# Start of a hybrid decoder layer: bias product and two more matmuls among the warm-up work, the later rows' norm right behind their sums, row copies on ScalarE, some low weights on GpSimd

## The chip, the cores and the metric

The kernel runs on one core of a Trainium2 chip. The metric is the time of one execution on the device in microseconds (us). The engines are TensorE (PE in the profile; PEld is its weight load), VectorE (DVE), ScalarE (ACT), GpSimd (POOL) and SyncE (SP), which issues most of the DMAs.

## The reference

One inference step of a decoder layer on 512 prompt rows and 32 sample rows (8 sequences of 4), each 1024 wide, in fp32:

```python
h = rmsnorm(x, norm_mix_pre)
xr, q, k, v, g = split(h @ w_in)              # 1024, 1024, 256, 256, 2048 columns
lru  = rg_lru(causal_conv4(xr))               # gated linear recurrence
attn = window_attention(q, k, v)              # window 128, 8 query heads, 2 kv heads, sinks,
                                              # relative bias rel_bias[bucket(distance)]
m = (sigmoid(g_lru) * (lru @ w_lru_o) + sigmoid(g_attn) * (attn @ w_attn_o)) @ w_out
x = x + rmsnorm(m, norm_mix_post)
u = causal_conv3(rmsnorm(x, norm_ffn_pre) @ w_up)
x = x + rmsnorm((gelu(u_gate) * u_val) @ w_down, norm_ffn_post)
```

It also returns the layer's states, among them the last 128 rows of `k` and `v`.

## The kernel before

Activations lie transposed, channels on the partitions and the 544 rows along the free axis, in two column halves: a = 0 is columns 0 to 255, a = 1 columns 256 to 543. Every fp32 product is made of three in a shorter format: each operand is split into a high and a low part (`hH`, `hL`; `wh`, `wl`), and `mm` multiplies high by high, high weight by low activation, and low weight by high activation. The high part is written by ScalarE, the low part is the difference, which VectorE makes as a rule. One product of 128 output channels takes 24 such matmuls.

A weight block of 1024 x 128 (`wload`, on SyncE's queue) is split in two halves of 128 x 512, called units; `wsplit_hi` (L278) and `wsplit_lo` (L283) make their parts. The helper `tick` orders the work around each product. Once per product it takes, in this order: the high parts of the next units (ScalarE), the side generators that are due (`sides`), the results of the product before (`todo`), the low parts of the units, and what stands in `last`. All engines work through what is issued to them in program order. `start_at(t, gen)` lets a generator begin at tick t; each `yield` ends its share of a tick.

How the kernel starts:

- SyncE loads the rows of `x` (five tiles of up to 128 rows, each in two halves of 512), gains and weights. The tables for the relative bias, `relx` (33 x 8) and the one-hot `ohp` (33 x 384), come behind the third weight block.
- TensorE runs WARM = 12 dummy products of `ones` and `ident`, transposes one gain vector (`ps_rows_a0`), and runs KEEP = 11 more dummies, while rows 0 to 255 of `x` arrive. `xsquares` sums their squares (ScalarE one half, VectorE the other), `xrstd` makes the reciprocal root of the mean with one Newton step on VectorE, `scale0` scales the rows.
- The rows are transposed into four PSUM tiles `ps_ta`; `hsplit` writes `hH` and `hL` from them, and the first product (`first_mm`, `pm_first`) follows piece by piece. Its two low weights are made by GpSimd.
- Then come products of the first five weight blocks with a = 0 (k and v of the first kv head, three query heads), and the same five with a = 1.
- The generator `norm_b` prepares the later rows, 256 to 543, from tick 1 on. In its first tick it puts `xsquares(2..4)` and the copies `keep_a(0..3)` into `last`; in its second `keep_a(4..7)`, `xrstd(2, 5)` and the scaling `xscale`; in its third and fourth it transposes into eight PSUM tiles `ps_tb`, and leaves `hsplit` and `keep_b` of each to the tick after. `keep_a` and `keep_b` copy the normed rows from PSUM to SBUF (`xn`), turn about on VectorE and ScalarE; the rows are needed again after the mixer.
- The generator `attn_tables` multiplies `relx` by `ohp` in tick 2 (`ps_ohp`), copies the result (`rvec`, VectorE) in tick 3 and writes it to DRAM (`rscr`, on GpSimd's DMA queue). `load_rep` replicates it in DRAM (`rrep`) for each pair of heads in ticks 4, 6, 13 and 20, and `load_btab` loads the skewed bias tables (`btab`) in ticks 5, 10, 17 and 26; both are issued by GpSimd.

Later, `v_done` (L692 to L694) copies each kv head's `v` from PSUM on ScalarE and its last 32 columns to `vn` on GpSimd; `sample_rows` transposes `kn` and `vn` (`pkn`, L778 and L779) in tick 19 for the attention of the sample rows. `put_away` writes `xn` to DRAM from GpSimd's queue from tick 13 on.

PSUM holds two pools of tiles of 128 x 512 floats: three for products (`PM`) and five for everything else (`PX`).

Of the kernel before, what the change touches and what calls it, by code (L numbers as in the profile page):

```python
# [11 lines left out]
F32 = mybir.dt.float32  # L12
# [5 lines left out]
P = 128  # L18
D = 1024
KD = D // P  # L20
SEQ = 512
# [3 lines left out]
NT = SEQ + NS  # L25
# [99 lines left out]
def hawk_step(ctx, tc, I, O):  # L125
# [69 lines left out]
    def tick(target=0, dt=1):  # L195
        now[0] += dt
        todo = late[:]
        late.clear()
        split = [wsplit_hi(u) for u in wclaim(target)]
        sides()  # L200
        for f in todo:
            f()
        for u in split:
            wsplit_lo(*u)
        for f in last:
            f()
        last.clear()
# [145 lines left out]
    def xload(i):  # L353
        t0, n, src = TOK[i]
        for z in range(2):
            xt[i, z] = S(f"x{i}_{z}")
            nc.sync.dma_start(out=xt[i, z][:n, 0:512], in_=src[:, 512 * z:512 * z + 512])

    xload(0)
    nc.sync.dma_start(out=rows_a[0:8, :], in_=I["norm_mix_pre"].rearrange("o (k p) -> (o k) p", p=P))  # L360
# [6 lines left out]
    wload(2)  # L367
    relx = cp.tile([NBK + 1, NH], F32, name="relx")
    pool.memset(relx, 1.0)
    nc.sync.dma_start(out=relx[0:NBK, :], in_=I["rel_bias"])  # L370
    ohp = T("ohp")[:NBK + 1, 0:3 * WIN]
    nc.sync.dma_start(out=ohp, in_=I["c_ohp"])
    for r, nme in ((8, "norm_mix_post"), (16, "norm_ffn_pre"), (24, "norm_ffn_post")):
# [4 lines left out]

    pw = PX("ps_warm")
    ps0 = PX("ps_rows_a0")  # L380
    for z in range(WARM):
        mm(pw[:, (z % 4) * P:(z % 4 + 1) * P], ones, ident, True, True)
    pe.transpose(ps0[:, 0:8], rows_a[0:8, :], ident[0:8, 0:8])
    for z in range(KEEP):
        mm(pw[:, (z % 4) * P:(z % 4 + 1) * P], ones, ident, True, True)
    G_PRE, G_POST, G_FPRE, G_FPOST, C_W, C_B, C_BR, C_BI, C_LAM = 0, 8, 16, 24, 32, 64, 72, 80, 88
# [69 lines left out]
    for z, k in enumerate(seq + (None,) * 3):  # L456
# [7 lines left out]
        if z == 1:  # L464
            wsplit_lo(*wsplit_hi(u1), eng=pool)
        if 2 <= z < KD + 2:
            first_mm(seq[z - 2], 0, 0, start=z == 2)
# [8 lines left out]
    rmsd = drp.tile([5, P], F32, name="rmsd")  # L476

    def keep_a(k):
        (dve.tensor_copy if k % 2 else act.copy)(xn[k][:, 0:256], ps_ta[k // 2][:, k % 2 * 256:k % 2 * 256 + 256])

    def keep_b(k, ps):
        (act.copy if k % 2 else dve.tensor_copy)(xn[k][:, 256:NT], ps[:, :288])

# [7 lines left out]
    def norm_b():  # L491
        last.extend(lambda i=i: xsquares(i) for i in (2, 3, 4))
        last.extend(lambda k=k: keep_a(k) for k in range(4))
        yield
        last.extend(lambda k=k: keep_a(k) for k in range(4, KD))
        last.append(lambda: xrstd(2, 5))
        last.extend(lambda i=i, e=e: xscale(i, e) for i, e in ((2, "av"), (3, "av"), (4, "vv")))
        yield
        for k in range(KD):
            ps = PX(f"ps_tb{k}")  # L500
            for i in (2, 3, 4):
                t0, n, _ = TOK[i]
                pe.transpose(ps[:, t0 - 256:t0 - 256 + n], xtile(i, k), ident[:n, :n])
            late.append(lambda k=k, ps=ps: (hsplit(k, 1, ps[:, :288]), keep_b(k, ps)))
            if k in (3,):
# [181 lines left out]
    def v_done(kv, a, ps):  # L687
# [5 lines left out]
        if a == 1:  # L693
            pool.tensor_copy(vn[:, kv, :], v[:, SEQ:NT])  # L694
            start_at(now[0] + 1, v_tok(kv, v))
# [266 lines left out]
    start_at(13, put_away())  # L962
    start_at(2, attn_tables())
    start_at(9, params())
# [933 lines left out]
```

## Time and profile before

| | |
|---|---|
| median of 3 runs | 1001.81 us (1001.38 to 1003.03) |
| the profiled execution | 1000.44 us |
| its span, first to last instruction | 998.6 us |
| TensorE busy in the span | 986.9 us |
| VectorE, ScalarE, GpSimd busy | 733.4, 578.1, 166.9 us |
| mean granted clock of TensorE | 0.999 |

The span is what the views of the profile divide up; 1.84 us of the execution lie outside it. Busy times overlap, so a busy engine need not set the time. In a row of the timeline the first figure is the start in us from the start of the span, the second the time until the end of the last instruction of the group (back-to-back instructions overlap, so starts tell the pace); then follow the engine, the line in the kernel, the operation, what it writes and reads, its size, the count, and in brackets the idle time ahead of it and what ended it. Line numbers are often those of a helper (L166 is every matmul made by `mm`), so the names tell the step.

### The profile page before, as it was taken

Reading aid. Unit: us, or ns where it says so; the run is one execution under the profiler, and the core shown is the slowest. Engines: PE = TensorE matmul, PEld = TensorE weight load, DVE = VectorE, ACT = ScalarE, POOL = GpSimd, SP = SyncE. Lnnn points to the kernel's source line nnn. Section 1 sums busy time; section 2 is a strip of 40 time slices with the busy share of each in tenths; the row PEclk is TensorE's granted clock in tenths of the full one; section 3 lists DMA queues with packets and bytes.
Section 4 is the critical chain, followed back from the end, with each engine's and each line's share of the span. In section 5 each row is a group of like instructions: output and inputs, shape, how many; then the busy total and the mean of one; then the engine's idle time right before and its main releaser. Section 6 shows DMA issues by size and latency. Waiting matters only on the chain.

```text
span 998.6 us, 20168 instructions
## 1 busy us (share of the span) xinstructions
PE 986.9 (99%) x7807; PEld 975.4 (98%) x7807; DVE 733.4 (73%) x1541; ACT 578.1 (58%) x1411; POOL 166.9 (17%) x279
## 2 busy tenths in 40 slices
PE   8999999999999999999999999999999999999997
PEld 7899999999999999999999999999999999999996
DVE  6566688545945656589777788888888888888765
ACT  6544455469448625556676756565656565656652
POOL 1152011001404463210001111111111111011004
PEclk9999999999999999999999999999999999999999
DMA  7756323322323634326256768676767676768612
GB/s 210 181 134 220 96 64 103 109 85 70 113 72 99 193 97 137 90 85 200 63 117 132 186 128 190 132 185 131 187 137 181 139 179 143 175 139 210 196 45 90
DMA packets 212114, 135.93 MB, mean 136 GB/s; under 512 B 9544, under 2 KB 197721, under 8 KB 211988
## 3 DMA queue, kind: packets, MB, share of 16 engines
q1 hardware_dynamic: 200052, 113.04, 39.8%
q0 software_dynamic: 11920, 19.59, 12.0%
q10 hardware_dynamic: 48, 2.03, 0.7%
q8 instruction: 61, 1.00, 0.4%
q14 instruction: 33, 0.27, 0.1%
HBM read 112.10 MB, written 11.37 MB: 124 GB/s over the span
## 4 chain that ended last, share of the span: by engine, by line
PE 92%; DVE 3%; ACT 3%; DMA 1%; issue 0%; SPq 0%; POOL 0%; ACTq 0%; DVEq 0%
PE pmin L166 21%; PE pmdn L166 17%; PE pux L1449 16%; PE puy L1449 8%; PE pq L1449 6%; PE pmout L166 5%; PE pmlo L166 5%; PE pmao L166 5%; PE puz L1449 4%; PE pg L166 1%; PE psc L166 1%; PE pvp L166 1%; PE pt L744 1%; PE ptok L166 1%; DMA x<-in_x_prompt_dram 1%; ACT wh_in L278 0%
## 5 line engine op out<-in xcount | busy, mean ns | idle before, releaser
L166 PE MATMUL pmin<-hH,wh_in 128*128 128x256 f32 (+1 forms) x568 | 166.0, 292 | 0.0
L166 PE MATMUL pmin<-hH,wl_in 128*128 128x256 f32 (+1 forms) x568 | 163.4, 288 | 0.4 <-DVE wl_in L283 0.4
L166 PE MATMUL pmin<-hL,wh_in 128*128 128x256 f32 (+1 forms) x568 | 163.7, 288 | 0.0
L166 PE MATMUL pmdn<-fH,wh_dn 128*128 128x256 f32 (+1 forms) x448 | 129.4, 289 | 0.2 <-DVE ft L175 0.2
L166 PE MATMUL pmdn<-fH,wl_dn 128*128 128x256 f32 (+1 forms) x448 | 129.1, 288 | 0.0
L166 PE MATMUL pmdn<-fL,wh_dn 128*128 128x256 f32 (+1 forms) x448 | 129.0, 288 | 0.0
L178 DVE SCALAR_TENSOR_TENSOR uc<-u,fv,uc 128x560 f32<-128x560 f32 x128 | 102.0, 797 | 13.3 <-ACT uc L1480 13.2
L166 PEld LDWEIGHTS pmin<-hH,wh_in 128*128 128x128 f32 x568 | 107.2, 189 | 1.9 <-issue 1.2
L166 PEld LDWEIGHTS pmin<-hH,wl_in 128*128 128x128 f32 x568 | 106.9, 188 | 0.7 <-DVE wl_in L283 0.6
L166 PEld LDWEIGHTS pmin<-hL,wh_in 128*128 128x128 f32 x568 | 107.0, 188 | 0.0
L166 PEld LDWEIGHTS pmdn<-fH,wh_dn 128*128 128x128 f32 x448 | 84.4, 188 | 0.6 <-issue 0.6
L166 PEld LDWEIGHTS pmdn<-fH,wl_dn 128*128 128x128 f32 x448 | 84.4, 188 | 0.0
L166 PEld LDWEIGHTS pmdn<-fL,wh_dn 128*128 128x128 f32 x448 | 84.4, 188 | 0.0
L1575 ACT COPY u<-pux 128x272 f32<-128x272 f32 x52 | 20.0, 385 | 83.8 <-PE pux L1449 83.8
L169 DVE TENSOR_TENSOR u<-puy,u 128x240 f32<-128x240 f32 (+2 forms) x78 | 24.6, 344 | 48.9 <-PE puy L1449 32.0
L175 DVE TENSOR_TENSOR ft<-ft,pmdn 128x256 f32<-128x256 f32 (+1 forms) x104 | 45.4, 437 | 17.0 <-PE pmdn L166 16.6
L278 ACT ACTIVATE wh_in<-raw_in 128x512 fp32r<-128x512 f32 x72 | 44.2, 628 | 17.6 <-PE pmin L166 6.1
L1480 ACT ACTIVATE uc<-u,fv 128x560 f32<-128x560 f32 x64 | 48.3, 755 | 0.0
L283 DVE TENSOR_TENSOR wl_in<-raw_in,wh_in 128x512 fp32r<-128x512 f32 x70 | 46.9, 684 | 0.8 <-ACT wh_in L278 0.7
L707 ACT ACTIVATE s<-s,st 128x256 f32<-128x256 f32 (+1 forms) x32 | 15.2, 475 | 50.1 <-DVE st L704 37.4
L1375 POOL DMA_DIRECT2D raw_up_s<-raw_up_s x26 | 22.7, 872 | 101.1 <-DMA raw_up_s<-raw_up__10513 4.5
L169 DVE TENSOR_TENSOR wl_dn<-raw_dn,wh_dn 128x512 fp32r<-128x512 f32 x56 | 38.4, 685 | 0.0
(782 smaller groups left out, 3427.6 us busy)
## 6 DMA issues: line engine op xcount, KB each, us to landing
raw_in<-in_w_in_dram SPq DMA_DIRECT2D x36, 512.0 KB
raw_dn<-in_w_down_dram SPq DMA_DIRECT2D x56, 256.0 KB
raw_up_s<-in_w_up_dram SPq DMA_DIRECT2D x25, 512.0 KB
raw_up_s<-raw_up_s POOLq DMA_DIRECT2D x26, 256.0 KB, 5.7
raw_ao<-in_w_attn_o_dram SPq DMA_DIRECT2D x8, 512.0 KB
raw_lo<-in_w_lru_o_dram SPq DMA_DIRECT2D x8, 512.0 KB
raw_out<-in_w_out_dram SPq DMA_DIRECT2D x8, 512.0 KB
xdram<-xn POOLq DMA_DIRECT2D x8, 272.0 KB, 14.0
```

The lines of the kernel that those rows point to most:

```text
L166: pe.matmul(out, l, r, start=start, stop=stop)
L169: dve.tensor_tensor(out=out, in0=a, in1=b, op=ALU.subtract)
L175: dve.tensor_tensor(out=out, in0=a, in1=b, op=ALU.add)
L178: dve.scalar_tensor_tensor(out=out, in0=a, scalar=s_, in1=b, op0=op0, op1=op1)
L278: act.activation(hl[0], raw, AF.Copy)
L283: (eng or dve).tensor_tensor(out=hl[1], in0=raw, in1=f32(hl[0]), op=ALU.subtract)
L707: act.activation(s3[:, j, :], s3[:, j, :], AF.Exp, bias=ng[:, j:j + 1], accum_out=sm[:, j:j + 1])
L744: pe.transpose(pt[:, (2 * ch + j) * P:(2 * ch + j + 1) * P], s3[:, j, ch * P:(ch + 1) * P], ident)
L1375: pool.dma_start(out=w["p4"], in_=w["p2"], accum_op=ALU.add)
L1449: pe.matmul(ps[:, :HN], w, x, start=start and k == 0 and i == 0, stop=stop and k == 3 and i == 2, skip_group_check=True)
L1480: act.activation(yt[j][:, 0:FLATU], u[:, 0:FLATU], AF.Copy, scale=fv[:, j:j + 1])
L1575: act.copy(e[nm_], z)
```

## The change

- The tables `relx` and `ohp` are loaded ahead of `x`, on ScalarE's DMA queue. Their product `ps_ohp` is issued right behind the gain transpose, ahead of the second group of dummies. The dummies' PSUM tile comes from the pool of products.
- Two more dummies are issued in the first product, ahead of its first matmul.
- In `norm_b`, `xrstd` and `xscale` move from the second tick to the end of the first, behind `keep_a(0..3)`. `attn_tables`, now a plain function, copies `rvec` on ScalarE and issues the write of `rscr` in the first tick as well, ahead of those copies.
- `keep_a` runs on ScalarE alone. `keep_b` runs after each group of four `hsplit`, the first two of a group on ScalarE and the other two on VectorE.
- In ticks 1 to 6 the second unit's low part is made by GpSimd.
- `vn` is copied by ScalarE.

```diff
@@ tick
-        for u in split:
-            wsplit_lo(*u)
+        for z, u in enumerate(split):
+            wsplit_lo(*u, eng=pool if z and now[0] <= 6 else None)
@@ the loads and the dummies
+    relx = cp.tile([NBK + 1, NH], F32, name="relx")
+    pool.memset(relx, 1.0)
+    act.dma_start(out=relx[0:NBK, :], in_=I["rel_bias"])
+    ohp = T("ohp")[:NBK + 1, 0:3 * WIN]
+    act.dma_start(out=ohp, in_=I["c_ohp"])
     xload(0)
...
     wload(2)
-    relx = cp.tile([NBK + 1, NH], F32, name="relx")
-    pool.memset(relx, 1.0)
-    nc.sync.dma_start(out=relx[0:NBK, :], in_=I["rel_bias"])
-    ohp = T("ohp")[:NBK + 1, 0:3 * WIN]
-    nc.sync.dma_start(out=ohp, in_=I["c_ohp"])
...
-    pw = PX("ps_warm")
+    pw = PM("ps_warm")
     ps0 = PX("ps_rows_a0")
+    def dummy(z):
+        mm(pw[:, (z % 4) * P:(z % 4 + 1) * P], ones, ident, True, True)
+
     for z in range(WARM):
-        mm(pw[:, (z % 4) * P:(z % 4 + 1) * P], ones, ident, True, True)
+        dummy(z)
     pe.transpose(ps0[:, 0:8], rows_a[0:8, :], ident[0:8, 0:8])
+    po = PX("ps_ohp")
+    mm(po[:NH, 0:3 * WIN], relx, ohp, True, True)
     for z in range(KEEP):
-        mm(pw[:, (z % 4) * P:(z % 4 + 1) * P], ones, ident, True, True)
+        dummy(z)
@@ the first product
+        if z == 2:
+            dummy(0)
+            dummy(1)
         if 2 <= z < KD + 2:
             first_mm(seq[z - 2], 0, 0, start=z == 2)
@@ the later rows
+    tb = []
     def keep_a(k):
-        (dve.tensor_copy if k % 2 else act.copy)(xn[k][:, 0:256], ...)
+        act.copy(xn[k][:, 0:256], ps_ta[k // 2][:, k % 2 * 256:k % 2 * 256 + 256])
     def keep_b(k, ps):
-        (act.copy if k % 2 else dve.tensor_copy)(xn[k][:, 256:NT], ps[:, :288])
+        (dve.tensor_copy if k % 4 > 1 else act.copy)(xn[k][:, 256:NT], ps[:, :288])
...
     def norm_b():
         last.extend(lambda i=i: xsquares(i) for i in (2, 3, 4))
+        last.append(attn_tables)
         last.extend(lambda k=k: keep_a(k) for k in range(4))
-        yield
-        last.extend(lambda k=k: keep_a(k) for k in range(4, KD))
         last.append(lambda: xrstd(2, 5))
         last.extend(lambda i=i, e=e: xscale(i, e) for i, e in ((2, "av"), (3, "av"), (4, "vv")))
+        yield
+        last.extend(lambda k=k: keep_a(k) for k in range(4, KD))
         yield
...
-            late.append(lambda k=k, ps=ps: (hsplit(k, 1, ps[:, :288]), keep_b(k, ps)))
+            late.append(lambda k=k, ps=ps: hsplit(k, 1, ps[:, :288]))
+            tb.append(ps)
+            if k % 4 == 3:
+                late.extend(lambda k=k, ps=tb[k]: keep_b(k, ps) for k in range(k - 3, k + 1))
@@ the bias table
     def attn_tables():
-        ps = PX("ps_ohp")
-        mm(ps[:NH, 0:3 * WIN], relx, ohp, True, True)
-        yield
         rvec = T("rvec")[:NH, 0:3 * WIN]
-        dve.tensor_copy(rvec, ps[:NH, 0:3 * WIN])
+        act.copy(rvec, po[:NH, 0:3 * WIN])
         pool.dma_start(out=rscr, in_=rvec)
-        yield
@@ v_done
-            pool.tensor_copy(vn[:, kv, :], v[:, SEQ:NT])
+            act.copy(vn[:, kv, :], v[:, SEQ:NT])
@@ the generators
-    start_at(2, attn_tables())
```

More of the change, by code (lines that the diff above doesn't have):

```diff
@@ L476, in hawk_step @@
     rmsd = drp.tile([5, P], F32, name="rmsd")
+    tb = []
     def keep_a(k):
-        (dve.tensor_copy if k % 2 else act.copy)(xn[k][:, 0:256], ps_ta[k // 2][:, k % 2 * 256:k % 2 * 256 + 256])
+        act.copy(xn[k][:, 0:256], ps_ta[k // 2][:, k % 2 * 256:k % 2 * 256 + 256])
     def keep_b(k, ps):
-        (act.copy if k % 2 else dve.tensor_copy)(xn[k][:, 256:NT], ps[:, :288])
+        (dve.tensor_copy if k % 4 > 1 else act.copy)(xn[k][:, 256:NT], ps[:, :288])
     def put_away():
@@ L492, in norm_b @@
         last.extend(lambda i=i: xsquares(i) for i in (2, 3, 4))
+        last.append(attn_tables)
         last.extend(lambda k=k: keep_a(k) for k in range(4))
+        last.append(lambda: xrstd(2, 5))
+        last.extend(lambda i=i, e=e: xscale(i, e) for i, e in ((2, "av"), (3, "av"), (4, "vv")))
         yield
         last.extend(lambda k=k: keep_a(k) for k in range(4, KD))
-        last.append(lambda: xrstd(2, 5))
-        last.extend(lambda i=i, e=e: xscale(i, e) for i, e in ((2, "av"), (3, "av"), (4, "vv")))
         yield
```

## The prediction

> **What bounds the kernel now.** I read first what TensorE waits for over the whole span, then the stretches of the first 90 us, then the start row by row.
>
> ```profile
> PE pkn L779 <- POOL vn L694: 1.2, 1, 1.2
> PE ps_tb L503 <- ACT x L422: 0.7, 2, 0.4
> PE pmin L166 <- DVE wl_in L283: 0.4, 1, 0.4
> ```
> ```profile
> 5.00:10.00 5.00, 5.00 (x33) 4.68 (x31) 1.94 (x9) 1.45 (x5) 0.00 (x0) 1.00 1.00 297
> ...
> 36.00:60.00 24.00, 24.00 (x190) 23.52 (x189) 13.28 (x40) 11.62 (x36) 5.92 (x20) 1.00 0.60 175
> 60.00:90.00 30.00, 30.00 (x243) 29.55 (x242) 19.14 (x56) 13.05 (x43) 9.69 (x32) 1.00 0.53 157
> ```
>
> The first view gives who waited for whom, then total, times and longest wait in us. The largest wait after the start is the one for `vn`, which GpSimd copies. The stretches (columns: length, then PE, PEld, DVE, ACT, POOL busy, clock, DMA share, GB/s) show no idle TensorE from 36 to 90 us. So a delay or a gain made before 36 us is carried to the end, and only two places matter: the start, and the `vn` wait near 91 us. All of the change lies in these two, save one 32-column copy near 45 us.
>
> I number the products: product 1 is the first (`pm_first`), products 2 to 5 follow in columns 0 to 255, one per tick, and product 6 is the first one on the later columns. Weight halves are u0, u1 (product 1), u2, u3 (product 2), and so on.
>
> ```profile
> 1.51 5.49 PE L166 MATMUL ps_warm<-ident,ones 128*128 128x128 f32 x24 [1.51 <-POOL relx L369]
> ...
> 7.13 1.09 PE L166 MATMUL ps_warm<-ident,ones 128*128 128x128 f32 x5
> 7.83 1.39 PE L166 MATMUL ps_warm<-ident,ones 128*128 128x128 f32 x11
> ```
> ```profile
> 16.99 0.28 PE L166 MATMUL pmin<-hH,wh_in 128*128 128x256 f32 x1
> ...
> 19.71 0.28 PE L166 MATMUL pmin<-hH,wl_in 128*128 128x256 f32 x1
> 19.92 0.81 PE L166 MATMUL ps_ohp<-ohp,relx 33*8 33x384 f32 x2
> 20.65 0.38 PE L166 MATMUL pmin<-hH,wh_in 128*128 128x256 f32 x1
> ...
> 21.07 0.38 PE L166 MATMUL pmin<-hH,wl_in 128*128 128x256 f32 x1
> ...
> 23.65 0.28 PE L166 MATMUL pmin<-hH,wl_in 128*128 128x256 f32 x1
> ...
> 27.03 0.39 PE L166 MATMUL pmin<-hH,wh_in 128*128 128x256 f32 x1
> ...
> 29.97 2.19 PE L503 MATMUL ps_tb<-ident,x 128*128 128x128 f32 x12
> 32.09 0.39 PE L166 MATMUL pmin<-hH,wh_in 128*128 128x256 f32 x1
> ...
> 35.71 0.30 PE L166 MATMUL pmin<-hH,wh_in 128*128 128x288 f32 x1
> ```
>
> First figure: start; second: time until the last of the group ends. Product 2 runs at (19.71 - 16.99)/23 = 0.118 us a matmul, 2.83 us in all, to 19.83. Then come the bias product (0.73, to 20.65), product 3 (to 23.77), twelve transposes, product 4 at 27.03, twelve transposes in 2.12 with nothing missing, product 5 at 32.09 and product 6 at 35.71. A product between transposes takes 29.97 - 27.03 = 2.94. So before product 4, 27.03 - 23.77 - 2.12 = 1.14 us are waiting (the `x` rows are scaled late), and product 5 has 3.62 - 2.94 = 0.68 of waiting (low weights).
>
> **Bias product among the dummies.** The dummies start at 7.13 at (1.09 - 0.27)/4 = 0.205 us each and from 7.83 on at (1.39 - 0.28)/10 = 0.111. Ahead of them the bias product costs 0.73 at full rate, and up to twice that while the rate is still halved. Taking the speed-up at the same time, its first half costs about 0.62 and its second 0.4, to 8.15; the 22 dummy passes then end at 8.15 + 22 x 0.111 = 10.6 instead of 9.97.
>
> ```profile
> 10.68 0.56 PE ps_ta L461 x3
> 11.32 0.85 ACT hH L432 x2
> ```
> ```profile
> 3.54 0.63 ACT L406 ACTIVATE jk<-x 128x512 f32<-128x512 f32 x1 [1.30 <-DMA x<-in_x_prompt_dram]
> ```
>
> In the chain, the second transpose starts at 10.68 when its rows are scaled. With the dummies to 10.6 it starts at about 10.8. The tables now loaded ahead of `x` (33 x 384 floats by the bias product's row, 51 KB) move those rows by 51 KB at 297 GB/s = 0.17 us at most, to 10.85. I take +0.2 for the whole chain behind it; ends 0 (loads overlap) and 0.5 (all at half rate). Issuing both loads on ScalarE's queue lies in its 1.30 us wait for `x`. SyncE's queue loses the same two issues, so that its later loads come earlier, and none of the engine rows shown here after 10 us waits for a load. The two more dummies cost 4 x 0.111 = 0.44 us, between the transposes and the first product, where TensorE waits for `hH` and `hL` anyway: the next transposes need `hL`, which moves by the same 0.2. Zero; without that cover, 0.44. At 20 us the bias product goes: -0.73 and the 0.09 around it, counted in the rebuild below.
>
> **Norm right behind the sums.** This is the decisive part, since ScalarE works in program order.
>
> ```profile
> 18.04 0.61 ACT L479 COPY xn<-ps_ta 128x256 f32<-128x256 f32 x2
> 18.55 1.15 ACT L278 ACTIVATE wh_in<-raw_in 128x512 fp32r<-128x512 f32 x2
> 19.61 0.36 ACT L642 ACTIVATE kH<-pm_first 128x256 fp32r<-128x256 f32 x1
> ...
> 22.45 0.30 ACT L390 ACTIVATE ss<-ss,epst 128x3 f32<-128x3 f32 x1 [1.98 <-DVE ss L175]
> 23.58 1.34 ACT L422 ACTIVATE x<-x,ss 128x512 f32<-128x512 f32 x2 [0.83 <-DVE ss L178]
> 24.82 1.13 ACT L278 ACTIVATE wh_in<-raw_in 128x512 fp32r<-128x512 f32 x2
> ```
> ```profile
> 18.86 0.07 DVE L408 DVE_READ_ACCUMULATOR jv<-x 32x1 f32 x1
> ...
> 20.00 0.42 DVE L169 TENSOR_TENSOR kL<-pm_first,kH 128x256 fp32r<-128x256 f32 x1 [0.40 <-ACT kH L642]
> 20.34 1.28 DVE L283 TENSOR_TENSOR wl_in<-raw_in,wh_in 128x512 fp32r<-128x512 f32 x2
> ```
>
> The high weights of u4, u5 (18.55) now stand behind the norm. On the old clock, without the 0.2: ScalarE's sums end at 18.04. The `rvec` copy there is new: 384 columns lie between one 256-wide copy (0.255, from 18.04 to 18.55 for two) and two; by columns 0.38. Four kept rows, 4 x 0.255 = 1.02, to 19.44. The square root starts there: VectorE's sums end before (18.86, less one low weight of 0.65 that leaves its queue). From it to the scaled rows 23.58 - 22.45 = 1.13, to 20.57, in which ScalarE idles. Two rows, 24.82 - 23.58 = 1.24, to 21.81. Then u4, u5 (1.06, to 22.87), `kH`, and 0.39 later `kL` (23.26), 0.34 later the low weights of u4 (23.60). From their start to the first matmul that uses them is 21.07 - 20.34 = 0.73: 24.33.
>
> TensorE needs u4 at 19.83 and gets only the two leading matmuls of product 3 in before 24.33: it stands idle for about 4.3 us. From there nothing is late. The rows are scaled by 22.2, so the 1.14 go; product 5's low weights come at about 32 and it starts at 34.2, so the 0.68 go. Rebuilt: 24.33 + 2.70 (rest of product 3, as from 21.07 to 23.77) + 2.12 + 2.94 + 2.12 + 2.94 = 37.15 for product 6, against 35.71. So **+1.44, with the 0.2: +1.64**. Each piece of ScalarE's chain may be off by a tenth; ends +1.0 and +2.3.
>
> **Low weights on GpSimd; kept rows on ScalarE.**
>
> ```profile
> 11.06 1.27 POOL L283 TENSOR_TENSOR wl_in<-raw_in,wh_in 128x512 fp32r<-128x512 f32 x1 [9.53 <-ACT wh_in L278]
> ```
> ```profile
> 312.29 1.13 POOL L915 TENSOR_TENSOR lt<-rg 128x568 f32<-128x568 f32 x1 [1.96 <-ACT rg L913]
> ...
> 314.86 1.44 POOL L915 TENSOR_TENSOR lt<-rg 128x568 f32<-128x568 f32 x1
> ```
> ```profile
> 314.62 0.68 DVE L283 TENSOR_TENSOR wl_in<-raw_in,wh_in 128x512 fp32r<-128x512 f32 x1
> ```
>
> The second halves (u3, u5, u7, u9) take 1.27 on GpSimd. Each is used twelve matmuls (1.4 us) after the first half's low weights, and u5 is ready at 22.97 + 1.3 = 24.3 against 24.33 + 1.4: hidden. GpSimd's queue ahead of them holds the `rscr` write, which waits for `rvec` to 18.4, and a table replication that waits for that write: both are over before u5 and u9. Beside a low weight on VectorE a GpSimd multiply took 1.44 instead of 1.13, and VectorE kept its 0.68, so GpSimd alone pays, 0.3 us, from slack. The Trainium skill (GPSIMD Engine Reference, Specifications) says that GpSimd shares its SBUF interfaces with VectorE and contends with instructions of two SBUF inputs, which these low weights are. If VectorE paid instead, its u4 would be late by up to 0.6 us, and the sum 0.6 higher; the trace speaks against it. The regrouped kept rows of the later columns shorten both queues after 28 us, where TensorE waits for neither any more: zero.
>
> **The `vn` copy on ScalarE.**
>
> ```profile
> 90.58 0.27 PE L778 MATMUL pkn<-ident,kn 128*64 128x128 f32 x1
> 92.09 0.30 PE L779 MATMUL pkn<-ident,vn 128*64 128x128 f32 x1 [1.25 <-POOL vn L694]
> 92.15 0.38 PE L166 MATMUL pmin<-hH,wh_in 128*128 128x288 f32 x1
> ```
> ```profile
> 90.94 0.74 POOL L624 DMA_DIRECT2D btab<-rrep  x1 [19.41 <-PE pkn L778]
> 91.67 0.37 POOL L694 COPY vn<-v 128x32 f32<-128x32 f32 x1
> ```
>
> The copy stands behind a bias-table load on which GpSimd has waited 19 us. On ScalarE it follows the `v` copy some 9 us earlier. The next product then starts at 90.58 + 2 x 0.11 = 90.80: **-1.35** (at least -1.25, the wait). Nothing else is late there; two small copies on ScalarE cost TensorE nothing.
>
> **Sum.** The profiled execution took 1000.44 us for a span of 998.6; +1.64 - 1.35 = +0.29, 1000.7. The median of the runs is 1001.81, 1.37 above it, so I forecast a median of **1002.1 us**, own range 1001.1 to 1003.2. About 0.2%, 2 us, is what a measurement of this kernel can tell from no change.
>
> **Rivals.**
> *The rate halves again (slower).* For 4.3 us TensorE would do only two matmuls. The dummies show that a rate of about one half exists (0.205 against 0.111, in a stretch whose granted clock reads 1.00), and that it held from the first dummy at 1.51 to 7.83, for 6.3 us. If the idle stretch brings it back, half of the slow time is lost: 3.1 us if it lasts as long as that, 2.1 if as long as the idle 4.3; 1004.2 to 1005.2. It decides once an idle stretch is long enough. Against it: two matmuls fall inside, and the transposes-only stretch from 23.77 to 27.03 brought no halving. The Trainium skill (TensorE: Matmul & The Clock Gate, What's actually happening) gives a free-running window of about 3.4 us, one idle window of which halves the clock until a busy one has passed. By that an estimate is 1.7 us, 1003.8, depending on where the window falls in the idle stretch; no trace shown here has such an idle window. Chance 0.22.
> *The order in the queue isn't what I read (faster).* If u4, u5 stay ahead of the norm, the 1.14, 0.68 and 0.82 of the start mostly go: about -2.4 + 0.2 - 1.35 = -3.6, 998.2. The trace of before follows program order throughout, which speaks against it. Chance 0.15.
> *The `vn` wait gives way to another* (the load, or the transposes behind it): +1.64, 1003.5. Chance 0.09.
> *VectorE pays for sharing, or `x` lands later by more than 0.2:* 1002.7 to 1003.2. Chance 0.09. The forecast itself keeps 0.45.
>
> **How the numbers follow.** Faster by over 2 us needs the second rival: 0.15 and 0.01 from tails, 0.16. Slower by over 2 us (above 1003.8): most of the first rival, 0.19; of the third a third, 0.03; tails of the forecast and the last rival, 0.08: 0.30. Within: 0.54. The range goes up to most of the first rival and down about two thirds of the way to the second: 999.6 to 1004.9.
>
> **What would show it.** Right: no `pkn` wait for `vn`; the bias product right behind the 8-row transpose; ScalarE with `x` ahead of the third pair of high weights; TensorE idle from about 20 to 24 us, waiting for `wh_in` and then `wl_in`; `ps_tb` without a wait; product 6 near 37.3. Wrong: product 6 before 36, matmuls of 256 columns 0.21 us apart after 24 us, or a new wait near 91.

## The result, and the profile after

The changed kernel takes 1011.63 us (median of 5 runs, 1009.99 to 1012.07) against 1001.38 us of the kernel before in the same comparison (5 runs, 1000.19 to 1003.03): ratio 1.0099, 95% interval 1.0084 to 1.0113. It is slower by about 10 us; forecast were 1002.1 us and a range of 999.6 to 1004.9. The profiled execution took 1009.99 us, its span 1007.9 us, 9.3 more than before.

The view of what TensorE waited for comes first, as for the kernel before (total, times, longest wait in us):

```profile
PE ps_ohp L166 <- DMA ohp<-in_c_ohp_dram: 4.8, 1, 4.8
PE pmin L166 <- ACT wh_in L278: 2.8, 1, 2.8
PE pmin L166 <- DVE wl_in L283: 1.9, 1, 1.9
```

The `pkn` wait for `vn` and the `ps_tb` waits are gone. The two `pmin` waits, 4.7 us together, are the stall that the prediction saw coming in front of product 3. The largest wait was in no step of the prediction: the bias product stood waiting for its table. The stretches (length, then PE, PEld, DVE, ACT, POOL busy, granted clock, DMA share, GB/s) say where the time went, and show a second thing:

```profile
0.00:16.00 16.00, 9.71 (x42) 8.25 (x42) 3.73 (x14) 4.41 (x10) 2.18 (x10) 0.79 0.81 245
16.00:36.00 20.00, 15.16 (x100) 14.04 (x100) 12.01 (x28) 14.37 (x37) 8.37 (x8) 0.84 0.59 161
36.00:60.00 24.00, 24.00 (x177) 22.28 (x176) 11.77 (x27) 13.52 (x34) 2.62 (x3) 0.99 0.46 131
60.00:90.00 30.00, 30.00 (x240) 29.08 (x239) 19.36 (x60) 11.70 (x40) 12.65 (x47) 1.00 0.49 135
```

From 36 us on TensorE is busy without a gap, as before. Ahead of that it lost time twice over: by waiting, and by a granted clock (the last column but two) below one, which the kernel before has at neither place. Row by row, the loads and the bias product first (start, time to the end; in brackets the idle time and what ended it):

```profile
4.04 4.84 SPq L357 DMA_DIRECT2D x<-in_x_prompt_dram  x4
4.54 0.41 ACTq L361 DMA_DIRECT2D relx<-in_rel_bias_dram  x1
6.20 0.54 ACTq L363 DMA_DIRECT2D ohp<-in_c_ohp_dram  x1
6.84 0.63 ACT L411 ACTIVATE jk<-x 128x512 f32<-128x512 f32 x1 [4.60 <-DMA ohp<-in_c_ohp_dram]
...
11.48 1.44 PE L166 MATMUL ps_ohp<-ohp,relx 33*8 33x384 f32 x2 [4.78 <-DMA ohp<-in_c_ohp_dram]
12.85 4.29 PE L166 MATMUL ps_warm<-ident,ones 128*128 128x128 f32 x22
...
23.36 0.28 PE L166 MATMUL pmin<-hH,wh_in 128*128 128x256 f32 x1
```

ScalarE had nothing to do from 2.24 us on, yet issued the loads at 4.54 and 6.20, and the one-hot table arrived after 11 us. Because TensorE works in order, the 22 dummy passes stood behind the bias product: they ended at 17.14 instead of the forecast 10.6, at 0.195 us a pass on average, since the rate had fallen during the wait (the granted clock reads 0.50 from 9.5 to 16.0 us). Product 2 starts at 23.36 instead of 16.99, 6.37 later.

Then the stall ahead of product 3 and what follows it:

```profile
29.13 0.39 PE L166 MATMUL pmin<-hH,wh_in 128*128 128x256 f32 x1 [2.79 <-ACT wh_in L278]
29.36 0.28 PE L166 MATMUL pmin<-hL,wh_in 128*128 128x256 f32 x1
31.56 0.58 PE L166 MATMUL pmin<-hH,wl_in 128*128 128x256 f32 x1 [1.93 <-DVE wl_in L283]
31.94 0.42 PE L166 MATMUL pmin<-hH,wh_in 128*128 128x256 f32 x1
32.16 0.41 PE L166 MATMUL pmin<-hL,wh_in 128*128 128x256 f32 x1
...
46.67 0.30 PE L166 MATMUL pmin<-hH,wh_in 128*128 128x288 f32 x1
```

Behind the stall the matmuls stand 0.21 us apart instead of 0.118. Product 6 starts at 46.67. From the start of product 2 to that of product 6 it is 23.31 us, 4.59 more than the 18.72 of before (35.71 - 16.99), where +1.44 had been worked out. The last row of the account is the `vn` transposes near 101 us:

```profile
101.56 0.27 PE L788 MATMUL pkn<-ident,kn 128*64 128x128 f32 x1
101.67 0.27 PE L789 MATMUL pkn<-ident,vn 128*64 128x128 f32 x1
```

They follow each other by 0.11 us; before it was 1.51. So the span grew by 6.37 + 4.59 - 1.4 = 9.6 by these rows, and by 9.3 as measured.

### The profile page after: what moved, and what is told of

The parts are those of the page before. It is cut to its first block, busy times and chain, and to the rows that moved or that the text cites. A ratio compares the mean times of both kernels' runs of the same rounds, so it can differ in the third digit from the quotient of the medians.

```text
span 1007.9 us, 20175 instructions
## 1 busy us (share of the span) xinstructions
PE 989.4 (98%) x7811; PEld 978.5 (97%) x7811; DVE 731.4 (73%) x1532; ACT 580.4 (58%) x1418; POOL 171.4 (17%) x281
## 4 chain that ended last, share of the span: by engine, by line
PE 93%; DVE 3%; ACT 2%; DMA 1%; issue 0%; SPq 0%; ACTq 0%; DVEq 0%
PE pmin L166 21%; PE pmdn L166 17%; PE pux L1458 15%; PE puy L1458 8%; PE pq L1458 6%; PE pmout L166 5%; PE pmlo L166 5%; PE pmao L166 5%; PE puz L1458 4%; PE pg L166 1%; PE psc L166 1%; PE pvp L166 1%; PE pt L754 1%; PE ptok L166 1%; DMA ohp<-in_c_ohp_dram 1%; PE ps_warm L166 0%
```

## The experiments

The table puts the runs side by side: median, ratio to the kernel before in the same comparison with its interval, and from each trace the start of product 2 and of product 6 (us).

| kernel | median | ratio | product 2 | product 6 | between |
|---|---|---|---|---|---|
| before | 1001.38 | 1 | 16.99 | 35.71 | 18.72 |
| the change | 1011.63 | 1.0099 (1.0084 to 1.0113) | 23.36 | 46.67 | 23.31 |
| a1_bias_back | 1002.76 | 1.0020 (1.0008 to 1.0031) | 16.81 | 39.53 | 22.72 |
| a2_norm_back | 1007.58 | 1.0068 (1.0053 to 1.0084) | 24.18 | 44.08 | 19.90 |
| a3_both_back | 999.71 | 0.9981 (0.9972 to 0.9991) | 16.97 | 36.52 | 19.55 |
| b1_vn_only | 999.31 | 0.9982 (0.9973 to 0.9991) | 17.22 | 35.94 | 18.72 |
| c1_tables_sync | 1011.95 | 1.0096 (1.0077 to 1.0116) | 25.10 | 48.81 | 23.71 |
| c2_tables_memset | 1002.88 | 1.0007 (0.9996 to 1.0017) | 16.38 | 39.72 | 23.34 |
| c4_tables_first | 1004.17 | 1.0015 (1.0003 to 1.0026) | 17.78 | 40.66 | 22.88 |
| c5_tables_gpsimd | 1003.74 | 1.0023 (1.0012 to 1.0034) | 17.10 | 40.34 | 23.24 |
| c6_tables_scalar_first | 1003.17 | 1.0016 (1.0004 to 1.0028) | 16.18 | 39.31 | 23.13 |
| c3_bridge | 1000.64 | 0.9988 (0.9975 to 1.0000) | 16.46 | 37.49 | 21.03 |
| d3_norm_only | 1002.17 | 1.0003 (0.9992 to 1.0015) | 17.24 | 38.65 | 21.41 |
| a5_low_on_vector | 997.66 | 0.9955 (0.9939 to 0.9971) | 15.98 | 33.88 | 17.90 |
| a6_vector_alternate | 998.37 | 0.9965 (0.9950 to 0.9979) | 16.95 | 34.99 | 18.04 |
| e3_kept_rows_late | 997.65 | 0.9955 (0.9939 to 0.9971) | 16.29 | 33.19 | 16.90 |
| f1_change_mended | 998.91 | 0.9963 (0.9949 to 0.9976) | 16.46 | 34.72 | 18.26 |

The median of the kernel before lay between 1001.24 and 1003.12 us in these comparisons, so the ratios are what can be compared from row to row. The start of product 2 hangs on when `x` lands and moves by over a microsecond from profile to profile where nothing waits for the tables (15.98 in a5, 17.24 in d3, whose code is the same up to there); the time between products 2 and 6 is the better measure of the steps behind it.

### Taking the parts back one by one

**a1: the bias part undone** (tables on SyncE behind the third weight block, product in tick 2), all else as changed:

```diff
-    act.dma_start(out=relx[0:NBK, :], in_=I["rel_bias"])   # ahead of x
+    nc.sync.dma_start(out=relx[0:NBK, :], in_=I["rel_bias"])  # behind wload(2), ohp too
-    mm(po[:NH, 0:3 * WIN], relx, ohp, True, True)          # ahead of the dummies
+    start_at(2, attn_tables())                              # product, rvec, rscr as before
```

> The changed kernel with its bias part undone: tables loaded by SyncE behind the third weight block, their product in tick 2 and the copy on VectorE in tick 3, as before; all else as changed. My theory: the 6.4 us by which product 2 starts later in the changed kernel (16.99 to 23.35) come from the wait for the table load and the half rate behind it, and go; the stall ahead of product 3 is the norm's own and stays (wh_in about 2 us, since the bias product fills part of it, then wl_in 1.9 us). Against before: +1.4 -1.35 = about 0 with TensorE at full rate behind the stall, +2.2 if it halves again (1001.4 to 1003.6). Rival: the stall and the halving at 30 us are a consequence of the late start; then product 3 does not wait and the time is 1.4 to 3 us under before.

Measured: product 2 at 16.81, ratio 1.0020. The bias part alone costs about 8 us of the 10. Product 2 to product 6 stays long, 22.72.

**a2: the norm back in the second tick**, bias part as changed:

```diff
         last.extend(lambda k=k: keep_a(k) for k in range(4))
-        last.append(lambda: xrstd(2, 5))
-        last.extend(... xscale ...)
         yield
         last.extend(lambda k=k: keep_a(k) for k in range(4, KD))
+        last.append(lambda: xrstd(2, 5))
+        last.extend(... xscale ...)
```

> The changed kernel with the norm and scaling of the later rows back in tick 2 behind the other four kept rows; the bias product stays among the dummies. My theory: product 2 still starts 6.4 us late; product 3 has no wait of over 0.5 us and no half rate, so of the 4.6 us lost between product 2 and product 6 all go; 1.1 us of waiting for scaled rows may come back. Time about 1011.6 - 4.6 = 1007, at least 4 us under the changed kernel. Rival (the stall comes from the shift of ScalarE's kept rows, not from the norm's place): product 3 waits as before, and the time stays at 1010 or more.

Measured: ratio 1.0068. Product 2 starts late as in the change (24.18), but the way to product 6 is 19.90 instead of 23.31. The norm's place is worth about 3.4 us. Two things were not as expected: product 3 still waits 1.91 us for a low weight, and the granted clock halves behind it (0.51 from 30.47 to 33.88 us), for half as long as in the change. So the 3.4 us hold waiting and rate together.

**a3: both undone.** What is left: low weights on GpSimd, `keep_a` and `keep_b` as changed, the dummies, `vn` on ScalarE.

> The changed kernel with both the bias part and the norm's place undone; what is left is the two dummies, the low weights on GpSimd, the kept rows on ScalarE and regrouped, and vn on ScalarE. My theory: no wait ahead of product 3, -1.35 us from vn, up to -0.7 from product 5's low weights: 999.3 to 1000.2 where before has 1001.4. Rival (GpSimd's low weights slow VectorE down by sharing, or ScalarE is now too full): at or above before.

Measured: ratio 0.9981. Of the 10 us nothing is left. Yet 19.55 us from product 2 to product 6 are 0.83 more than before: something in the remainder still costs. Product 3, which was expected not to wait, waits 1.02 us for a low weight, and the granted clock halves behind that (0.50 from 22.27 to 25.68 us).

**b1: the kernel before with `vn` on ScalarE alone.**

```diff
-            pool.tensor_copy(vn[:, kv, :], v[:, SEQ:NT])
+            act.copy(vn[:, kv, :], v[:, SEQ:NT])
```

> The kernel before with only the vn copy moved to ScalarE. My theory: the wait of 1.25 us ahead of the second pkn transpose goes and nothing takes its place: -1.35 us, ratio 0.9987, span about 997.2. Rival: the bias-table load behind which the copy stood, or the transposes behind it, hold TensorE at the same place: no change.

Measured: ratio 0.9982 (0.9973 to 0.9991), 1.8 us; the span is 997.4, 1.2 less than before, 1.4 if product 6, which starts 0.23 later here, is taken as the mark. Nothing took the place of the `vn` wait.

### Why the tables were late

**c1: both tables on SyncE's queue ahead of `x`.**

```diff
-    act.dma_start(out=relx[0:NBK, :], in_=I["rel_bias"])
+    nc.sync.dma_start(out=relx[0:NBK, :], in_=I["rel_bias"])
     ...
-    act.dma_start(out=ohp, in_=I["c_ohp"])
+    nc.sync.dma_start(out=ohp, in_=I["c_ohp"])
```

> The changed kernel with one edit: the two tables are loaded ahead of x by SyncE instead of ScalarE. Theory 1 (ScalarE's loads were issued late, at 4.5 and 6.2 us, behind 2 MB that SyncE had asked for already): from SyncE they land before the first dummies end, the bias product does not wait, the half rate from 9 to 16 us goes, and product 2 starts at 17.0 to 17.6 instead of 23.35; the stall ahead of product 3 stays. Time 1002.5 to 1005.5 against 1011.6. Theory 2 (the DMA engines are full, so that the tables land late from any queue, or x lands late in their place): the wait for the tables or for x stays over 2 us and the time at 1008 or more.

Measured: 1011.95 us, no better. The trace shows that the edit did not do what was meant:

```profile
0.74 0.42 SPq L363 DMA_DIRECT2D ohp<-in_c_ohp_dram  x1
...
7.86 0.36 SPq L361 DMA_DIRECT2D relx<-in_rel_bias_dram  x1
```

The one-hot table went first, but the load of `relx` went out at 7.86 us, behind five half tiles of `x` and two weight loads, and TensorE waited 5.9 us for it. The queue's order is not the order of the source lines here; `relx` is filled by GpSimd ahead of its load, which the other loads are not. So this run told nothing about the theories.

**c2: no loads at all**, both tables filled with ones by GpSimd (the values of the relative bias are left out):

```diff
-    act.dma_start(out=relx[0:NBK, :], in_=I["rel_bias"])
-    act.dma_start(out=ohp, in_=I["c_ohp"])
+    pool.memset(ohp, 1.0)
```

> The changed kernel with both tables of the bias product filled with ones by GpSimd instead of loaded, so that they are there before the first dummy (the values of the relative bias are left out). If the place of the bias product is cheap and only the landing of its tables was late, there is no wait ahead of it, the 22 dummy passes end near 10.6 us, product 2 starts at 16.8 to 17.4 us, and the rest is as in the kernel with the bias part undone (22.7 us from product 2 to product 6): 1002.0 to 1003.5 us. If the bias product costs by its place, because it breaks the run of dummies and the rate falls again, the passes stay near 0.2 us each and the time is above 1006.

Measured: no wait, the 22 passes in 2.72 us at full rate, product 2 at 16.38, 1002.88 us. The place of the bias product costs nothing that shows; the landing of its tables is the whole of the 6.4 us ahead of product 2. With product 2 in time the rest is as in the change: 23.34 from product 2 to product 6.

**c4: real tables, loaded by SyncE as its very first loads** (c1's edit), with only the last row of `relx` filled, so that its load waits for nothing:

```diff
-    pool.memset(relx, 1.0)
+    pool.memset(relx[NBK:NBK + 1, :], 1.0)
```

> The changed kernel with both tables loaded by SyncE ahead of the first rows of x, and only the table's last row filled by GpSimd, so that neither load waits for anything. If the late landing was the fault, the tables land before 7 us, TensorE doesn't wait ahead of the bias product, and x comes later by the two issues, up to 0.8 us: product 2 at 17.2 to 18.3 us and 1002.5 to 1004.5 us in all. If the tables are slow to land wherever they are issued, the wait ahead of the bias product stays at 3 us or more and the time above 1007.

Measured: issued at 0.74 and 1.17 us, no wait, 1004.17 us. Product 2 at 17.78: `x` comes behind two more issues.

**c6: the same two loads as ScalarE's first instructions; c5: on GpSimd's queue.**

```diff
+    act.dma_start(out=relx[0:NBK, :], in_=I["rel_bias"])    # c6, with c4's fill
+    act.dma_start(out=ohp, in_=I["c_ohp"])
     act.activation(warm, epst, AF.Sqrt)
...
-    act.dma_start(...)                                      # c5: both
+    pool.dma_start(...)
```

> The changed kernel with the two table loads as ScalarE's very first instructions, ahead of its activation table and the first square root, and with only the table's last row filled by GpSimd. If ScalarE's loads were late because they were issued behind SyncE's first six (SyncE had issued 1.0 MB by the time the changed kernel's first table load went out at 4.54 us), they go out near 0.74 and 1.2 us here and land before 7 us: no wait ahead of the bias product, product 2 at 17 to 18.5 us, 1003 to 1005 us as with SyncE's loads ahead of x. If ScalarE's queue is slow whenever it shares with SyncE's, the second load is issued after 4 us and lands after 9 us, the wait ahead of the bias product stays at 2 us or more, and the time is above 1006.

> The changed kernel with the two table loads on GpSimd's queue, right behind its fill of the table at 1.5 us. If the issue behind SyncE's loads is what held them, they wait here as on ScalarE, land near 11 us, and the time is 1010 to 1012. If it was ScalarE's queue, they land before 8 us, with no wait ahead of the bias product: product 2 at 16.5 to 17.5 us and 1002 to 1004 us.

ScalarE's and TensorE's rows in c6, then GpSimd's and TensorE's in c5:

```profile
0.75 0.42 ACTq L350 DMA_DIRECT2D relx<-in_rel_bias_dram  x1
1.20 0.61 ACTq L352 DMA_DIRECT2D ohp<-in_c_ohp_dram  x1
...
6.28 0.81 PE L166 MATMUL ps_ohp<-ohp,relx 33*8 33x384 f32 x2
```
```profile
1.84 0.70 POOL L361 DMA_DIRECT2D relx<-in_rel_bias_dram  x1 [0.31 <-POOL relx L360]
2.54 0.56 POOL L363 DMA_DIRECT2D ohp<-in_c_ohp_dram  x1
...
7.12 0.80 PE L166 MATMUL ps_ohp<-ohp,relx 33*8 33x384 f32 x2 [0.21 <-DMA ohp<-in_c_ohp_dram]
```

From ScalarE at 0.75 and 1.20 the tables are there in time. From GpSimd, at the time when ScalarE could have issued them in the change, they go out at once and land just about in time (4.4 us for the one-hot table). In the change the one-hot table took about 5.2 us from its issue at 6.20 to 11.4, not much more than c5's 4.4: it was late because it was issued late. And that was not ScalarE's queue as such: an issue by ScalarE is held once SyncE's loads are under way, one by GpSimd, at 1.84 and 2.54, is not. (By 4.54 us SyncE had issued four half tiles of `x` and two weight blocks, 2 MB, not the 1.0 MB of the expectation of c6.) GpSimd's fill of `relx`, which c4 and c6 changed too, is no other explanation: it ended at 1.53 us, before ScalarE was free, and the one-hot load, which needs no fill, went out 1.25 us after the load before it (4.95 to 6.20). SyncE's own issues are held as well: its load of `x` at 4.04 took 3.41 us to issue where the ones ahead took some 0.4, and in c2, without any table load, 2.88. In the profile's queue table c5's loads are a queue of their own (software), while SyncE's and ScalarE's are both of the hardware kind. What the two share, and what holds them, the runs don't show.

### What made the way to product 6 so long

**c3: a1 with 12 dummies ahead of product 3's first matmul**, to keep TensorE at work while it waits:

```diff
     for z, c in enumerate(qkv_order[:FIRST]):
+        if z == 2:
+            for d in range(12):
+                dummy(d)
         step(("in", c), h, 0, ...
```

> As a1_bias_back, with 12 more dummy products on TensorE right ahead of product 3, where it stands idle for 2.06 us waiting for high weights. They add no work that anything needs. If the granted clock halves because TensorE does too little in some 3.4 us (it read 0.50 from 22 to 28.7 us in a1_bias_back), the rest of product 3 runs at 0.12 us a matmul instead of 0.21 and the time falls by about 2 us, to 1000.5 to 1001. If the half rate has another cause, or the dummies only delay product 3: no change or up to 0.7 us slower than a1_bias_back's 1002.8.

The stretches of a1, then of c3:

```profile
20.00:24.00 4.00, 1.33 (x4) 0.50 (x2) 2.85 (x10) 3.31 (x8) 0.86 (x1) 0.75 0.19 51
24.00:28.00 4.00, 2.99 (x14) 2.99 (x15) 2.02 (x3) 2.77 (x7) 2.53 (x4) 0.50 0.17 37
```
```profile
20.00:24.00 4.00, 3.55 (x27) 3.05 (x26) 2.92 (x8) 3.66 (x10) 1.21 (x1) 1.00 0.19 55
24.00:28.00 4.00, 3.33 (x26) 3.13 (x27) 1.67 (x3) 2.46 (x7) 2.25 (x4) 1.00 0.14 26
```

The clock stays at 1.00, the way to product 6 shrinks by 1.69 us (22.72 to 21.03), and the ratio goes from 1.0020 to 0.9988. Work that computes nothing made the kernel about 2 to 3 us faster, because it kept the rate. The halving is a cost of its own, besides the waiting. Product 3's first low-weight matmul comes as late as in a1 (8.21 and 8.20 us after the start of product 2); from it to product 6 it is 12.82 us (24.67 to 37.49) instead of 14.52, and 12.82 is what the prediction had added up for full rate (37.15 - 24.33).

**d3: a1 with all low weights on VectorE**: the early norm and `vn`, without GpSimd.

```diff
-        for z, u in enumerate(split):
-            wsplit_lo(*u, eng=pool if z and now[0] <= 6 else None)
+        for u in split:
+            wsplit_lo(*u)
```

> The changed kernel with the bias part undone and the low weights all on VectorE: the early norm is left, with the vn copy. If VectorE pays for sharing with GpSimd, the sums of VectorE take 0.69 us again, the norm comes 0.5 us earlier and the low weight after it 0.6 us earlier: product 2 to product 6 takes 20.2 us as the prediction's sum had it if the clock stays whole, up to 21.7 if it halves once more; 1000.0 to 1001.8 us. If the sharing costs nothing and the half rate alone made the difference, it is 22.5 us and more from product 2 to product 6, and 1002.5 us.

Measured: 21.41 from product 2 to product 6, 1.31 less than a1, 1002.17 us, ratio 1.0003. The first low-weight matmul of product 3 comes at 24.36, 7.12 after product 2's start; the prediction had 24.33 - 16.99 = 7.34. The 7.34 hold 0.38 for the `rvec` copy on ScalarE, which d3 leaves to VectorE; without it the sum is 6.96, so the early norm by itself was sized right to within 0.2 us. In a1 the same matmul comes 8.20 after product 2's start, so GpSimd's low weights cost 1.08 there. The rate halves all the same; the two stretches of 3.4 us ahead of it and behind it:

```profile
22.25:25.65 3.40, 1.80 (x13) 1.59 (x14) 2.39 (x6) 3.40 (x11) 0.00 (x0) 1.00 0.18 46
25.65:29.05 3.40, 3.40 (x18) 3.01 (x16) 0.91 (x2) 1.03 (x3) 1.58 (x2) 0.50 0.49 124
```

**a5: a3 with all low weights on VectorE.** (Same edit.)

> As a3_both_back, with all low weights of the first ticks on VectorE again as before. In a3_both_back VectorE's sums (jv, 0.69 us alone) took 1.80 us and its low weights 1.26 instead of 0.68 while GpSimd made a low weight at the same time. If VectorE pays for the sharing, these return to 0.69 and 0.68, the wait of 1.02 us for wl_in ahead of product 3 shrinks to about 0.5 (the kept rows on ScalarE remain), and the half rate from 22 to 25.5 us may go with it: 0.5 to 2.2 us faster than a3_both_back's 999.7. If the slowness came from something else in those ticks (the kept rows, the accumulators), the durations stay and the time rises, since VectorE has more to do.

Measured: 17.90 from product 2 to product 6 against 19.55 of a3, 997.66 us, ratio 0.9955. The wait ahead of product 3 shrinks from 1.02 to 0.45, and the granted clock stays at 1.00, so the difference holds the halved rate of a3 as well. Who paid for GpSimd's help is seen in the rows around the same sum of squares, first in the change (VectorE, GpSimd), then in a5 (VectorE, GpSimd idle):

```profile
22.77 1.80 DVE L413 SCALAR_TENSOR_TENSOR jv<-x 128x512 f32<-128x512 f32 x1
24.50 0.68 DVE L413 SCALAR_TENSOR_TENSOR jv<-x 128x512 f32<-128x512 f32 x1
...
22.73 1.29 POOL L283 TENSOR_TENSOR wl_in<-raw_in,wh_in 128x512 fp32r<-128x512 f32 x1 [2.17 <-ACT wh_in L278]
```
```profile
16.00 0.68 DVE L411 SCALAR_TENSOR_TENSOR jv<-x 128x512 f32<-128x512 f32 x1
```

VectorE's sum began 0.04 us behind GpSimd's subtraction and took 1.80 instead of 0.68: it ended 0.55 us after GpSimd (24.02), as if it had hardly started until GpSimd was done. GpSimd kept its 1.29. The same happens to the low weight that product 3 waits for, shown in a1 (VectorE, GpSimd):

```profile
23.71 1.25 DVE L283 TENSOR_TENSOR wl_in<-raw_in,wh_in 128x512 fp32r<-128x512 f32 x1
...
23.14 1.27 POOL L283 TENSOR_TENSOR wl_in<-raw_in,wh_in 128x512 fp32r<-128x512 f32 x1 [5.66 <-ACT wh_in L278]
```

In d3, where GpSimd makes none, two such low weights take 1.28 together.

### Towards a better version

**a6: a5 with the kept rows of the early columns turn about on VectorE and ScalarE again.**

```diff
-        act.copy(xn[k][:, 0:256], ...)
+        (dve.tensor_copy if k % 2 else act.copy)(xn[k][:, 0:256], ...)
```

> The version with bias part and norm as before and all low weights on VectorE, and with the kept rows of the early columns alternating between VectorE and ScalarE again: what is left of the change is the regrouped kept rows of the later columns, two dummies and the vn copy. If ScalarE's kept rows were worth something in that version, product 2 to product 6 goes from 17.9 us back towards 18.7 and the time to 998.5; if they were not, it stays at 997.3 to 998.0.

Measured: 18.04 from product 2 to product 6, ratio 0.9965 against a5's 0.9955, intervals overlapping. ScalarE's kept rows are worth 0.14 us by the traces, nothing that the times can tell.

**e3: a5 with the bias product inside the first product, its tables loaded by SyncE behind the second tile of `x`, all `keep_a` in the second tick and no extra dummies.**

```diff
-        last.extend(lambda k=k: keep_a(k) for k in range(4))
         yield
-        last.extend(lambda k=k: keep_a(k) for k in range(4, KD))
+        last.extend(lambda k=k: keep_a(k) for k in range(KD))
...
+        if z == KD:
+            po.append(PX("ps_ohp"))
+            mm(po[0][:NH, 0:3 * WIN], relx, ohp, True, True)
```

> A version built from the findings: the kernel before, with vn on ScalarE, kept rows of the earlier columns all in tick 2 on ScalarE ahead of the norm (behind the third pair of high weights), the later kept rows regrouped as in the change, all low weights on VectorE, and the bias product inside the first product where TensorE waits for hH and hL (tables loaded by SyncE behind the first 256 rows of x). Expected against before: -1.35 (vn), -0.7 (product 5's low weights), -0.5 to -1.1 (rows scaled earlier), -0.8 (bias product hidden): 997.3 to 998.5, if TensorE's clock stays at full rate; 1.7 us more if it halves once.

Measured: the shortest way to product 6, 16.90, and no gain in the time, 997.65: from product 6 to the end of the span it takes 962.6 us (995.8 - 33.19) against a5's 961.3 (995.2 - 33.88), so it gives back 1.3 us behind that point. Most of it goes far from the change: at the first matmul that writes `puy`, in the feed-forward part, e3 is still 0.4 us ahead of a5 (522.5 against 522.9), at the last that writes `pux` 0.5 behind (941.9 against 941.4), with no wait of TensorE in between in either trace. Why is left open; a5's profile is of the fastest of its four runs, so part of it may be scatter.

**f1: the change with its three faults mended** (c6's loads, norm in the second tick, low weights on VectorE):

> The changed kernel with three things mended: the tables loaded by ScalarE's first instructions, the norm back in the next tick, all low weights on VectorE. What is left: the bias product among the dummies, kept rows on ScalarE, the vn copy. If the three were the whole of the loss, there is no wait of more than 0.5 us ahead of products 3 to 6 and no halving of the rate behind the dummies; product 2 to product 6 takes 17.1 us (17.9 of the kernel with bias part and norm undone and all low weights on VectorE, less the 0.82 that the bias product took at 20 us), product 2 starts at 16.2 to 17.2 us, and the time is 996.0 to 997.8 us, ratio 0.994 to 0.997. If something else of the change costs time, it is 998 us or more.

Measured: ratio 0.9963 (0.9949 to 0.9976), in the expected interval, though the median, 998.91 us, is above the expected times (the kernel before took 1003.12 in this comparison); and the way to product 6 is 18.26, not 17.1. The waits of TensorE in f1:

```profile
PE pmin L166 <- DVE wl_in L283: 1.3, 1, 1.3
PE ps_ta L466 <- DVE x L447: 0.3, 1, 0.3
PE ps_tb L514 <- ACT x L427: 0.2, 1, 0.2
```

In a5 the first of them is 0.4. There the bias product fills TensorE's time in front of product 3 while the low weight is being made; taken away from that place, it leaves a wait of the same size. So the early bias product, even with its tables in time, gains nothing at 20 us. a5, e3 and f1 all beat both kernels; a5, which leaves the bias product where it was, is as good as any.

## Why the prediction was wrong, point by point

**Bias product among the dummies, +0.2: the step that failed.** Measured +6.37 on the start of product 2. The prediction looked at the engine, ScalarE's 1.30 us of waiting for `x`, and took for granted that an engine with time to issue gets its load issued and that 51 KB land with the first rows. It priced the load by its bytes (0.17 us) and gave no end of the range to its landing, which takes 4.4 us even when the issue goes out at once (c5). The issue was held until 4.54 and 6.20 us and the table came after 11; with the tables in time (c2, c6) product 2 starts at 16.38 and 16.18. The cover that the step named, that the issue lies in ScalarE's wait, was looked up on the engine, not on the queue. With the tables mended and all else as changed, the kernel takes 1002.9 to 1004.2 us (c2, c4, c5, c6): the late tables alone took the result out of the range.

**Norm right behind the sums, +1.44: mechanism right, two terms missing.** ScalarE's order was as forecast row by row, TensorE stood idle first for `wh_in`, then for `wl_in`, 4.72 us against 4.3, and `ps_tb` waits no more. The first low-weight matmul came 8.20 us after product 2's start (31.56 - 23.36) against 7.34 worked out: +0.86, which is VectorE's sharing with GpSimd. Of that 0.59 is u4's low weight: its first matmul comes 1.32 us after it starts (30.24 to 31.56) instead of 0.73, beside a low weight that GpSimd began at 29.69. The other 0.27 lie in the chain ahead of it, where VectorE's sums ended late. From there to product 6 it was 15.11 against 12.82: +2.29, which is the halved rate, since at full rate (c3) it is 12.82. 1.44 + 0.86 + 2.29 = 4.59, as measured.

**The rate halves again, given 0.22: it happened.** It was the only way named in which the matmuls would stand 0.21 us apart, and the price of 2.1 to 3.1 us holds the 2.29. The argument against it was wrong: two matmuls in the stall don't prevent it, and the stretch with transposes only, which the prediction leaned on, was no safe precedent, being busier (2.69 us of the 3.4 us up to 27.00). The Trainium skill (TensorE: Matmul & The Clock Gate, What's actually happening) has the rate halve after an idle window of some 3.4 us. The lengths agree: the slow stretches last 3.4 us in d3 (25.65 to 29.05) and close to twice that in the change. What it says of the trigger, idle, is too narrow for d3, where TensorE was busy for 1.80 of the 3.4 us ahead of the halving, and for a3, where one wait of 1.02 us came ahead of it and TensorE was busy for 2.39 of the 3.41 us up to 22.27. Busy time alone doesn't decide either: in f1, with a wait of 1.34 us and 1.93 us busy of the 3.40 from 18.15 to 21.55, the rate stayed whole. What does, the runs don't show.

**Low weights on GpSimd, zero: wrong, and the row was misread.** The prediction saw a GpSimd multiply take 1.44 instead of 1.13 beside a VectorE low weight and concluded that GpSimd alone pays. In that row VectorE had started first (314.62 against 314.86). Here GpSimd started first (22.73 against 22.77) and VectorE paid, 1.12 us. The low weights of a1 are a third such pair (23.14 and 23.71). The rows agree with one rule: who starts second waits. The Trainium skill (SBUF — State Buffer, SBUF: two separate sides) states just that: the ports that the two engines share are an exclusive lock, held by whichever starts first for its whole instruction. The prediction had gone by another page of the Trainium skill, and had priced u4's low weight at up to 0.6 us in a rival with 0.09; that price was right (0.59), but VectorE's sums and the halved rate behind the longer wait were not in it. From a3 to a5, the halved rate of a3 included, it is 1.65 us on the way to product 6, and the medians differ by 2.05 us.

**The `vn` copy, -1.35: right.** 1.51 us between the two transposes became 0.11, and b1 alone is faster by 1.8 us (ratio 0.9982), nothing else being late there.

**The two more dummies, kept rows: zero, as far as seen.** a6 against a5 is 0.14 us. The dummies were not tried by themselves.

**The rival "order in the queue"** did not come about: the engines did follow program order. On SyncE's DMA queue, in c1, the order was another than in the source.

The two places add up and don't feed each other: with the tables in time (c2) the way from product 2 to product 6 is 4.62 us longer than before, with the tables late 4.59.

## What to carry to other kernels

A load that is moved has to be priced by when it lands, and that by what is already under way on the queues at its time of issue; a small table that heads a chain belongs ahead of the large loads, or on a queue that they don't use, and TensorE must not stand in order behind a load whose landing no row shows. A stall of TensorE of one to a few microseconds can cost more than its length, since the rate can halve behind it (1.02 us was enough in a3, 1.34 did nothing in f1): either fill it with matmuls that compute nothing or don't make it. When work goes to GpSimd, compare the start times in the rows before deciding who pays; in the three pairs of rows here the engine that started second did, and if that is the busy one, the help costs more than it brings.

## What the runs showed of the hardware

- ScalarE, free from 2.24 us, issued its loads at 4.54 and 6.20 while SyncE's loads were under way; GpSimd issued the same loads at 1.84 and 2.54, and ScalarE at 0.75 and 1.20 when it came first. A single load of SyncE took 3.41 us to issue in that stretch (from 4.04), others some 0.4.
- TensorE's rate halved after a 3.4 us stretch with 1.80 us of busy time (d3), and stayed at half for 3.4 us of unbroken work. It also halved behind a stretch of 3.41 us with 2.39 busy (a3), and not behind one of 3.40 with 1.93 (f1). Twelve dummies in the gap kept it whole (c3).
- A VectorE operation with both inputs in SBUF that starts 0.04 us behind a GpSimd subtraction takes 1.80 instead of 0.68 us, GpSimd's own time being unchanged (1.29).
